# Hybrid attention block on one core: the second pass's weights in a layout of their own, and the lower right input block freed at the turn

## The chip, the cores and the metric

The kernel runs on one core of a Trainium2 chip. The metric is device time in microseconds (us) of one execution; lower is better. Engines are named as the profile names them: PE is TensorE's matmul, PEld its weight load, DVE is VectorE, ACT ScalarE, POOL GpSimd, and SP is SyncE, whose queue issues all of the DMAs that this text is about. A queue is worked off in order: an instruction that waits holds up all that stand behind it on its engine.

## What is computed

One layer of a streaming encoder, batch 1, 2048 positions, model width 1024, all in float32. Of the reference, what matters here is the first product; everything behind it uses its pieces:

```
xn = rms_norm(h, norm_gain[layer])
proj = xn @ w_in[layer]
qa, ka, va, ga, qb, kb, vb, gb, iq, ik, iw, za, zb = jnp.split(proj, offsets, axis=-1)
ya = chunked_relpos_attention(qa, ka, va, rel_bias[layer]) * jax.nn.silu(ga)
yb = dsa_sparse_attention(qb, kb, vb, iq, ik, iw) * jax.nn.silu(gb)
merged = gate_a * (ya @ w_branch_a[layer]) + gate_b * (yb @ w_branch_b[layer])
h = h + merged @ w_out[layer]
```

`x` is 2048 by 1024 and `w_in` some 5,500 columns wide. The branches a (banded attention) and b (top-256 attention) follow, and an output product.

## The kernel before

**Arithmetic.** Every float32 factor is split into a high part (rounded to the PE's fp32r) and a low part, and a product is three matmuls: high by high, high by low, low by high (`mm3`, L218 records them all). The split costs an ACT copy and a subtraction on DVE or POOL for each tile of weights.

**Stages.** Up to about 600 us the first half of the columns, the normalisation and the index branch run. From about 610 us to about 1090 us follow the *seven-product units*: 18 units (`quads`) of 256 output columns, each for the two remaining groups of 512 positions. The input is seen as a 2 by 2 matrix of blocks, A11, A12 (one group of positions, lower and upper half of the 1024 inputs), A21, A22 (the other group), and the weights of a unit as 2 by 2 blocks too. Seven block products in place of eight give the result. A block product is four slices `k` of three matmuls, 12 matmuls of 128x128 by 128x512.

- The **first pass** (`prep_one`, `first_half`) does four products of every unit, with A11, A21, A12 and A22, and keeps three sums of each unit in DRAM (`qD`).
- At the **turn** the input blocks are combined in place: A21 becomes A22 minus A21 (four slices, within the last unit of the first pass), then A22 becomes A21 plus A11 (four slices), both on PE (`combine_pe`, L1239: four matmuls by plus or minus the identity into PSUM, an ACT copy for the high part at L1241, a DVE subtraction for the low part at L1242). A12 becomes A12 minus A21 on POOL, DVE and ACT (`combine`, L1218 to L1222).
- The **second pass** (`prep_two`, `load_sums`, `part`) does three products of every unit, 36 matmuls, adds the sums from DRAM (L1367) and stores results (`evac`, L692, L698, L719).

**Weights on their way.** Per unit and slice `k` the four 128x128 blocks come by DMA to a staging tile (`wst` or `wst2`, four to five buffers), POOL combines them in place (L1260 to L1262, or L1349 and L1350), ACT writes the high part (L1248), DVE the low part (L1249). DRAM holds the weights as `wP[unit, half of the columns, 128, 8 row tiles, 128]`; a staging tile takes two DMAs, one for each half of the columns. In the second pass only three blocks are needed, one from the first half (L1347, 64 KB) and two from the second (L1348, 128 KB).

**Memory.** The second pass's pool `w2` (the sums `part`, tags p0 to p2 with two buffers each; the weights `wt2`, three buffers; staging `wst2`, four) is opened where pool `xA` and the first pass's weights lay. `xA` holds one input block, A11, so whatever lies there waits until A11 has been read for the last time, by the fourth slice of A21 plus A11. With two buffers for each sum, the sum of unit n can only be loaded when that of unit n-2 has been stored.

**Order.** The program text gives dependencies and a rough order; the order on each engine is then set by a list scheduler at build time, so an edit moves instructions that it doesn't name. After the second pass come the attention units (`a_unit`, `b_unit`), of which the first few are interleaved with the last units of the second pass, then the branch products and the output product.

## Time and profile before

| | us |
|---|---|
| median of 3 runs (2096.8 to 2107.16) | 2101.71 |
| the profiled execution | 2098.61 |
| its span, first to last instruction | 2096.8 |
| PE busy in it | 2000.5 (95%) |
| ACT, DVE, POOL busy | 1267.2, 1479.2, 804.8 |
| DMA queues' packets, share of 16 engines | 55.8% |

PE is busy 95% of the span, so what can be won is mostly the 5% in which it waits, and the stretches in which its clock was granted below full. Both are gathered in a few places, which the windows of the profile show. A busy PE in these rows also covers matmuls stretched by the low clock or by the start after an idle time, so the number of matmuls in a window, times the pitch of an undisturbed row of them, says better what was lost.

### The profile page before, as it was taken

The numbers are of one execution on the slowest core, as the hardware profiler recorded it, in microseconds if no ns is written. First come the engines' busy times: TensorE is split into PE (matmuls) and PEld (weight loads), VectorE is DVE, ScalarE is ACT, GpSimd is POOL, SyncE is SP. The second block draws the span as 40 slices with busy tenths as digits, with TensorE's granted clock in tenths as the row PEclk, the third lists the DMA queues.
The fourth block names the chain that finished last, engine by engine and source line by source line (L and its number), as shares of the span: only waits on it lengthen the run. The fifth ranks groups of instructions, "written<-read, shape, count | busy, mean of one in ns | idle before, by whom it ended". The sixth has DMA issues, their size and how long they took to land.

```text
span 2096.8 us, 34363 instructions
## 1 busy us (share of the span) xinstructions
PE 2000.5 (95%) x10674; PEld 1687.6 (80%) x10674; DVE 1479.2 (71%) x3646; ACT 1267.2 (60%) x2484; POOL 804.8 (38%) x1043
## 2 busy tenths in 40 slices
PE   8799999999999999999888999999999999999998
PEld 7588878889889877766666888888888898887886
DVE  6748887969789986565456668766885688775444
ACT  5456565565566563344567678867896698873221
POOL 2122223321142455444324455445444544443410
PEclk9899999999999999999999999999999999999999
DMA  9473345364464665478889764556346632145642
GB/s 354 150 233 130 119 133 168 115 208 152 161 209 130 221 208 187 150 245 276 253 288 252 221 212 149 182 187 216 111 133 191 212 119 68 56 138 185 215 141 91
DMA packets 310541, 375.78 MB, mean 179 GB/s; under 512 B 34384, under 2 KB 185296, under 8 KB 310224
## 3 DMA queue, kind: packets, MB, share of 16 engines
q1 hardware_dynamic: 310352, 373.54, 55.8%
q8 instruction: 85, 1.39, 0.3%
q14 instruction: 104, 0.85, 0.1%
HBM read 252.88 MB, written 120.55 MB: 178 GB/s over the span
## 4 chain that ended last, share of the span: by engine, by line
PE 43%; DMA 7%; ACT 3%; DVE 3%; issue 2%; POOL 2%; SPq 1%; DVEq 0%; POOLq 0%; ACTq 0%
PE po L1432 8%; PE d L218 7%; PE O L1015 6%; PE s L990 5%; PE pt L1007 5%; PE acc L218 4%; PE O L925 3%; PE pt L915 2%; PE s L880 2%; DMA wst<-wP 2%; DMA dst<-wB 1%; DMA dst<-wA 1%; DVE P L811 1%; DMA bias<-biasD 0%; DMA sg<-gAD 0%
## 5 line engine op out<-in xcount | busy, mean ns | idle before, releaser
L218 PE MATMUL acc<-xh,wt 128*128 128x512 f32 x2160 | 700.2, 397 | 22.9 <-ACT wt L1248 12.3
L218 PEld LDWEIGHTS acc<-xh,wt 128*128 128x128 f32 x2160 | 405.5, 189 | 126.3 <-ACT wt L1248 19.2
L218 PE MATMUL acc<-xl,wt 128*128 128x512 f32 x1080 | 425.1, 394 | 0.0
L832 POOL TENSOR_TENSOR ptl<-pf,pth 128x512 fp32r<-128x512 f32 (+1 forms) x144 | 179.7, 1248 | 207.4 <-ACT pf L828 146.8
L218 PEld LDWEIGHTS acc<-xl,wt 128*128 128x128 f32 x1080 | 204.2, 189 | 43.2
L835 DVE TENSOR_TENSOR ptl<-pt,pth 128x512 fp32r<-128x512 f32 (+1 forms) x288 | 187.5, 660 | 50.9 <-ACT pth L834 50.1
L210 POOL TENSOR_TENSOR wt<-wst,wt 128x512 fp32r<-128x512 f32 (+1 forms) x92 | 118.0, 1309 | 270.3 <-ACT wt L209 241.7
L487 DVE SCALAR_TENSOR_TENSOR sc<-lg,iw,sc 128x512 f32<-128x512 f32 (+2 forms) x266 | 178.9, 679 | 42.8 <-ACT lg L482 37.6
L990 PE MATMUL s<-kBt,qsB 128*128 128x512 f32 (+3 forms) x640 | 187.7, 383 | 1.0 <-DVE mx L811 0.7
L482 ACT ACTIVATE lg<-lg 128x512 f32<-128x512 f32 (+2 forms) x304 | 149.8, 524 | 63.7 <-PE lg L480 62.2
L834 ACT ACTIVATE pth<-pt 128x512 fp32r<-128x512 f32 (+1 forms) x288 | 160.7, 578 | 26.3 <-PE pt L1007 13.3
L1007 PE MATMUL pt<-ident,P 128*128 128x128 f32 x1088 | 165.4, 273 | 1.0 <-DVE ptl L835 0.5
L993 ACT ACTIVATE P<-P,mx 128x128 f32<-128x128 f32 (+15 forms) x128 | 154.4, 1209 | 19.5 <-DVE mx L811 19.2
L1015 PE MATMUL O<-pth,vBt 128*128 128x256 f32 x544 | 146.9, 288 | 4.0 <-ACT pth L834 1.9
L1015 PE MATMUL O<-ptl,vBt 128*128 128x256 f32 x544 | 148.0, 298 | 1.2 <-POOL ptl L832 0.8
L811 DVE CUSTOM_DVE_ANT_0 P<-s,mk,mx 128x512 f32<-128x512 f32 (+2 forms) x192 | 125.2, 652 | 32.0 <-PE s L990 25.3
L1007 PEld LDWEIGHTS pt<-ident,P 128*128 128x128 f32 x1088 | 128.3, 141 | 9.2 <-ACT pf L828 1.4
L1248 ACT ACTIVATE wt<-wst 128x512 fp32r<-128x512 f32 (+1 forms) x144 | 76.4, 571 | 94.2 <-POOL wst L1350 48.8
L1053 POOL TENSOR_TENSOR dw<-dst,dw 128x512 fp32r<-128x512 f32 x64 | 83.2, 1301 | 124.9 <-ACT dw L1052 112.8
L1249 DVE TENSOR_TENSOR wt<-wst,wt 128x512 fp32r<-128x512 f32 (+1 forms) x144 | 95.2, 684 | 48.7 <-ACT wt L1248 43.1
L880 PE MATMUL s<-kk,qs 128*128 128x320 f32 (+1 forms) x448 | 108.3, 339 | 7.5 <-DVE mx L811 4.6
L218 PE MATMUL d<-ya,dw 128*128 128x512 f32 x384 | 108.2, 407 | 6.2 <-ACT dw L1052 5.8
(274 smaller groups left out, 4453.8 us busy)
## 6 DMA issues: line engine op xcount, KB each, us to landing
wst<-wP SPq DMA_DIRECT2D x224, 128.0 KB
wst<-wP SPq DMA_DIRECT2D x84, 256.0 KB
qs<-qA SPq DMA_DIRECT2D x128, 128.0 KB
kk<-kA SPq DMA_DIRECT2D x56, 256.0 KB
vs<-vA SPq DMA_DIRECT2D x56, 256.0 KB
qD<-q SPq DMA_DIRECT2D x54, 256.0 KB
part<-qD SPq DMA_DIRECT2D x54, 256.0 KB
bias<-biasD SPq DMA_DIRECT2D x32, 320.0 KB
```

Of the source, the lines that this page charges most:

```text
L218: nc.tensor.matmul(acc, a, b, start=(first and i == 0), stop=(last and i == n - 1), **({} if first and last else {"skip_group_check": True}))
L482: nc.scalar.activation(lg, lg, AF.Relu)
L487: nc.vector.scalar_tensor_tensor(o_, lg, wv, o_, op0=OP.mult, op1=OP.add)
L832: nc.gpsimd.tensor_tensor(lo, pf, f32(hi), op=OP.subtract)
L834: nc.scalar.activation(hi, src, AF.Copy)
L835: nc.vector.tensor_tensor(lo, src, f32(hi), op=OP.subtract)
L880: nc.tensor.matmul(s_ps[:, :w], q[:, m, j * 128:(j + 1) * 128], kk[:, ko:ko + w], start=(m == 0), stop=(m == 1))
L990: nc.tensor.matmul(s_ps[:, :w], q[:, h, :], kBt[:, m, a:a + w], start=(m == 0), stop=(m == 1))
L993: nc.scalar.activation(P[:, e, :n], P[:, e, :n], AF.Exp, bias=mx[:, e:e + 1], scale=-1.0, accum_out=st["sum"][:, (u % 2) * 2 + e:(u % 2) * ...
L1007: nc.tensor.transpose(pt[:, k, e, :], P[:, e, (kt + k) * 128:(kt + k + 1) * 128], ident)
L1015: nc.tensor.matmul(o_, vBt[:, kt + k, :], src[:, k, :], start=(kt + k == 0 and n_ == 0), stop=(kt + k == b and n_ == 1), skip_group_check= ...
L1432: nc.tensor.matmul(accs[t, hf], a, b[:, n_], start=(k == 0 and i == 0), stop=(k == KT - 1 and i == 2))
```

## The change

Three things are done together.

1. A second copy of the seven-product units' weights is laid out on the host, `wS[unit, slice k, 128, 4 blocks, 128]`: what one staging tile takes is 128 rows of 2 KB, side by side, in the order block 1, 0, 2, 3 of before. One DMA fills a staging tile in the first pass, and one of 128 rows of 1.5 KB (the last three blocks) in the second.
2. The pool `xA`, whose place is given up at the turn, holds A22 in place of A11. A21 plus A11 is written over A11, and the second product of the second pass reads A11 for A22.
3. The four slices of A21 plus A11 stand behind `part(0, 0)`, the first product of the second pass, in the text, and no longer ahead of opening `w2`.

```diff
-    parts = {(s, h, z): (apool if s + h == 0 else xpool).tile([128, 4, 512], F32R, name=f"x{z}{s}{h}")
+    parts = {(s, h, z): (apool if s + h == 2 else xpool).tile([128, 4, 512], F32R, name=f"x{z}{s}{h}")
...
-            for c in range(2):
-                nc.sync.dma_start(st[:, 2 * c:2 * c + 2], io["wP"][u, c, :, k::4, :])
+            nc.sync.dma_start(st, io["wS"][u, k])
             e.tensor_tensor(st[:, 2], st[:, 3], st[:, 2], op=OP.subtract)
-            e.tensor_tensor(st[:, 3], st[:, 2], st[:, 0], op=OP.add)
-            e.tensor_tensor(st[:, 3], st[:, 1], st[:, 3], op=OP.subtract)
+            e.tensor_tensor(st[:, 3], st[:, 2], st[:, 1], op=OP.add)
+            e.tensor_tensor(st[:, 3], st[:, 0], st[:, 3], op=OP.subtract)
...
-        product(a, W, 0, A11, True, False)
+        product(a, W, 1, A11, True, False)
...
-        product(a, W, 1, A12, False, True)
+        product(a, W, 0, A12, False, True)
...
-            nc.sync.dma_start(st[:, 0:1], io["wP"][u, 0, :, k:k + 1, :])
-            nc.sync.dma_start(st[:, 1:3], io["wP"][u, 1, :, k::4, :])
+            nc.sync.dma_start(st, io["wS"][u, k, :, 1:4])
...
-        mm3(acc, [((W[z][:, 0, k], W[z][:, 1, k]), (A21, A22, A12)[z](k)) for k in range(4)], z == 0, z == 2)
+        mm3(acc, [((W[z][:, 0, k], W[z][:, 1, k]), (A21, A11, A12)[z](k)) for k in range(4)], z == 0, z == 2)
...
-    for k in range(4):
-        combine_pe(A22, A21, A11, 0, k, 2)
     a_st.close()
...
     part(0, 0)
+    for k in range(4):
+        combine_pe(A11, A21, A11, 0, k, 2)
```

**Where the order moves: ACT at the turn.** Names: `xh10` is A21's high part, `xh11` A22's, `xh00` A11's, `xh01` A12's; `wt2` are the second pass's weights, numbered by unit. ACT before:

```order
L1241 ACTIVATE xh10_146<-cm_8981 128x512
L1221 ACTIVATE xh01_144<-ct_9163 128x512
L1241 ACTIVATE xh11_148<-cm_9021 128x512
L1241 ACTIVATE xh11_148<-cm_9042 128x512
L1241 ACTIVATE xh11_148<-cm_9035 128x512
L1248 ACTIVATE wt2_9065<-wst_9066 128x3x128
L1248 ACTIVATE wt2_9065<-wst_9073 128x3x128
L1248 ACTIVATE wt2_9065<-wst_9080 128x3x128
L1248 ACTIVATE wt2_9065<-wst_9087 128x3x128
L1248 ACTIVATE wt2_9094<-wst_9095 128x3x128
```

and ACT now:

```order
L1241 ACTIVATE xh00_142<-cm_9048 128x512
L1221 ACTIVATE xh01_144<-ct_9076 128x512
L1248 ACTIVATE wt2_8965<-wst_8966 128x3x128
L1248 ACTIVATE wt2_8965<-wst_8972 128x3x128
L1248 ACTIVATE wt2_8965<-wst_8978 128x3x128
L1248 ACTIVATE wt2_8965<-wst_8984 128x3x128
L1248 ACTIVATE wt2_8990<-wst_8991 128x3x128
L1241 ACTIVATE xh10_146<-cm_8909 128x512
L1241 ACTIVATE xh00_142<-cm_9055 128x512
```

The five copies that make the first weights of the second pass stood behind all eight combined slices; now they stand ahead of the last slice of A21 (`cm_8909`) and the last two of A11.

**PE at the same place.** `cm` is a combined slice in PSUM, `acc_9123` and `acc_9015` are the first product of the second pass. PE before:

```order
L1239 MATMUL cm_9042<-xl00_143,unit_8958 128x512
L1239 MATMUL cm_9035<-xh10_146,unit_8958 128x512
L1239 MATMUL cm_9035<-xl10_147,unit_8958 128x512
L1239 MATMUL cm_9035<-xh00_142,unit_8958 128x512
L1239 MATMUL cm_9035<-xl00_143,unit_8958 128x512
L218 MATMUL acc_9123<-xh10_146,wt2_9065 128x512
L218 MATMUL acc_9123<-xl10_147,wt2_9065 128x512
```

and PE now:

```order
L1239 MATMUL cm_9055<-xl00_143,unit_8886 128x512
L1239 MATMUL cm_9062<-xh10_146,unit_8886 128x512
L218 MATMUL acc_9015<-xh10_146,wt2_8965 128x512
L218 MATMUL acc_9015<-xl10_147,wt2_8965 128x512
L218 MATMUL acc_9015<-xh10_146,wt2_8965 128x512 x2
L218 MATMUL acc_9015<-xl10_147,wt2_8965 128x512
L218 MATMUL acc_9015<-xh10_146,wt2_8965 128x512 x2
L218 MATMUL acc_9015<-xl10_147,wt2_8965 128x512
L218 MATMUL acc_9015<-xh10_146,wt2_8965 128x512 x2
L218 MATMUL acc_9015<-xl10_147,wt2_8965 128x512
L218 MATMUL acc_9015<-xh10_146,wt2_8965 128x512
L1239 MATMUL cm_9062<-xl10_147,unit_8886 128x512
```

The twelve matmuls of the first product stood behind the last combined slice; now they stand between the first and the second matmul of that slice.

**SP's queue in the second pass.** `part` are the sums, loaded from `qD` and later stored from the same tile to `sBD`, `sAD`, `kA` and others. SP before, from the stores of the sixth and seventh unit on:

```order
L698 DMA sBD2_96<-part_9541 128x512
L1357 DMA part_9704<-qD4_112 128x512
L1357 DMA part_9705<-qD4_112 128x512
L1347 DMA wst2_9729<-wP 128x128
L1348 DMA wst2_9729<-wP 128x2x128
L1357 DMA part_9706<-qD4_112 128x512
L719 DMA kA3_67<-eh_9723 128x512
L719 DMA kA3_67<-part_9621 128x512
L1347 DMA wst2_9736<-wP 128x128
L1348 DMA wst2_9736<-wP 128x2x128
L1347 DMA wst2_9743<-wP 128x128
L1348 DMA wst2_9743<-wP 128x2x128
```

and SP now, at the like place:

```order
L1355 DMA part_9598<-qD4_112 128x512
L719 DMA kA3_67<-part_9517 128x512
L698 DMA sAD3_93<-part_9597 128x512
L1355 DMA part_9680<-qD5_113 128x512
L1355 DMA part_9757<-qD6_114 128x512
L1346 DMA wst2_9701<-wS 128x384
L1346 DMA wst2_9707<-wS 128x384
L719 DMA kA2_66<-eh_9674 128x512
L1346 DMA wst2_9713<-wS 128x384
L1346 DMA wst2_9719<-wS 128x384
L719 DMA kA2_66<-part_9518 128x512
L698 DMA sAD3_93<-part_9679 128x512
```

A unit's weights take four places in place of eight, and the loads of sums have moved closer to the stores that free their tiles: before, `part_9706` takes the home of `part_9541`, five places behind that one's store; now `part_9680` and `part_9757` take the homes of `part_9517` and `part_9597`, each two places behind the store.

## Rows read from the trace of the kernel before

**Rows 1.** The page: each engine's busy time, share of the span, instructions.
```profile
PE 2000.5 (95%) x10674; PEld 1687.6 (80%) x10674; DVE 1479.2 (71%) x3646; ACT 1267.2 (60%) x2484; POOL 804.8 (38%) x1043
```

**Rows 2.** Windows: stretch, its length, busy us (and instructions) of engines.
```profile
core 0: us, PE busy (x) PEld busy (x) DVE busy (x) ACT busy (x) POOL busy (x), PEclk, DMA share, GB/s
600.00:870.00 270.00, 262.23 (x1286) 221.40 (x1285) 214.39 (x471) 137.64 (x246) 132.34 (x235) 0.99 0.59 192
870.00:910.00 40.00, 33.12 (x121) 23.62 (x120) 30.68 (x44) 14.31 (x27) 15.60 (x22) 0.91 0.44 145
910.00:1020.00 110.00, 102.26 (x425) 79.23 (x423) 56.23 (x91) 48.37 (x84) 45.94 (x92) 0.98 0.84 266
1020.00:1105.00 85.00, 71.33 (x321) 53.15 (x322) 44.31 (x107) 59.57 (x116) 27.11 (x40) 0.96 0.89 276
1105.00:1180.00 75.00, 63.82 (x368) 53.50 (x368) 46.55 (x153) 55.08 (x155) 34.30 (x41) 0.93 0.94 248
1180.00:2097.00 917.00, 893.19 (x5427) 777.93 (x5425) 624.29 (x1677) 609.66 (x1186) 399.69 (x366) 1.00 0.49 155
```

**Rows 3.** Timeline of PE at the turn: start, length, instruction, idle before it.
```profile
879.65 0.40 PE L1239 MATMUL cm<-xh,unit 128*128 128x512 f32 x1
...
894.09 0.47 PE L218 MATMUL acc<-xh,wt 128*128 128x512 f32 x1 [1.50 <-ACT wt L1248]
...
902.59 0.50 PE L218 MATMUL acc<-xh,wt 128*128 128x512 f32 x1 [1.22 <-ACT wt L1248]
```

**Rows 4.** Timelines of ACT and SP at the turn.
```profile
893.12 2.17 ACT L1248 ACTIVATE wt<-wst 128x384 fp32r<-128x384 f32 x5
892.39 2.88 SPq L1357 DMA_DIRECT2D part<-qD  x6
```

**Rows 5.** Timeline of SP in the second pass.
```profile
915.29 1.24 SPq L1357 DMA_DIRECT2D part<-qD  x2
...
945.29 0.38 SPq L1347 DMA_DIRECT2D wst<-wP  x1
945.71 0.55 SPq L1348 DMA_DIRECT2D wst<-wP  x1
947.13 0.33 SPq L1357 DMA_DIRECT2D part<-qD  x1
...
1008.90 2.10 SPq L1357 DMA_DIRECT2D part<-qD  x2
```

**Rows 6.** Waits of SP's queue from 910 to 1020 us: total, times, longest.
```profile
SPq L1357 <- DMA sBD<-part: 2.7, 4, 0.9
SPq L1357 <- DMA sAD<-part: 2.5, 3, 2.0
SPq L1357 <- DMA qB<-part: 1.9, 2, 1.1
...
SPq L1357 <- DMA kA<-part: 1.1, 1, 1.1
```

**Rows 7.** The chain that ended last, in order of time: start, us, what.
```profile
924.15 2.93 DMA sBD<-part
...
971.29 3.87 DMA kA<-part
...
999.75 4.73 DMA sAD<-part
...
1005.88 3.06 DMA wst<-wP
...
1009.10 0.47 POOL wst L1349
...
1010.13 0.53 ACT wt L1248
...
1989.29 99.17 PE po L1432 x432
```

**Rows 8.** Windows again: the first 50 us, columns as in group 2.
```profile
0.00:50.00 50.00, 42.16 (x244) 37.18 (x244) 30.16 (x70) 29.81 (x62) 10.40 (x110) 1.00 0.94 351
```

## What the change would do, predicted before it ran

> **What bounds the kernel now.** I read the page's busy line first, to see which engine could set the time at all. PE is busy 95% of the span, DVE 71%, ACT 60% [rows 1]. PE does the same matmuls after the change as before, since the seven products and the eight combined slices stay. So only time in which PE waits, or runs at a low clock, can be won. The windows say where that is [rows 2]. The last one, from 1180 us to the end, has PE busy 893.19 of 917 us at a clock of 1.00, on attention and output products, and the change does not touch them. From 600 to 870 us, the first pass, PE is busy 262.23 of 270. The three windows between are worse: 33.12 of 40 at the turn (clock 0.91), 102.26 of 110 in the second pass (clock 0.98), 71.33 of 85 in its end. That is about 7, 8 and 14 us of idle time, and none is on PE's own account.
>
> The turn, first. PE's timeline shows eight combined slices from 879.65 us on and then the first product at 894.09, which waited 1.50 us for its weights on ACT, and the second at 902.59, which waited 1.22 for the same [rows 3]. SP's timeline gives the reason: the first loads into the new pool start at 892.39 [rows 4], when A11 has been read for the last time, and every weight of the second unit is queued behind them.
>
> The second pass, next. A unit needs 36 matmuls. An undisturbed row of the same shape late in the kernel took 99.17 us for 432 [rows 7], which is 0.23 us each, so PE needs 8.3 us for a unit. SP's timeline shows pairs of loads of sums at 915.29 and at 1008.90, and ten units lie between [rows 5]: 93.61 / 10 = 9.36 us. So something holds each unit 1.1 us longer than PE needs. SP's row of issues is nearly unbroken there: two DMAs of a weight tile at 945.29 and 945.71 take 0.38 and 0.55 us, the next load of a sum 0.33 [rows 5], and SP's waits, nearly all for stores to land so that a load may take their tile, are 2.7, 2.5, 1.9 and 1.1 us in the whole window, 8.2 of 110 [rows 6]. The chain that ended last goes the same way: it runs through landings of stores (2.93, 3.87, 4.73 us), then a weight DMA of 3.06, a POOL subtraction of 0.47 and an ACT copy of 0.53 [rows 7]. I therefore read the pass as bound by SP's queue, not by the amount of data: the windows have the DMA engines at 266 GB/s and a share of 0.84 there [rows 2], and the first 50 us reached 351 GB/s at 0.94 [rows 8].
>
> **The change part by part.** *Weights in one DMA, second pass.* A unit issued four pairs, 4 x (0.38 + 0.55) = 3.7 us of SP [rows 5]. Now it issues four single DMAs of 128 rows. No row shows such a DMA for three blocks. The nearest are the two that it replaces: 0.38 for 128 rows of one block and 0.55 for 256 pieces [rows 5]. I take 0.47, the middle, so 1.9 us a unit, and keep 1.5 (4 x 0.38) and 2.2 (4 x 0.55) for the range. SP's own work falls by 1.5 to 2.2 us a unit, 1.8 by my value, so from 9.36 less its waits of 8.2/11 = 0.7 (eleven to twelve units lie in the window) = 8.6 to 6.8 us.
>
> That is not the new period, since the loads of sums now stand two to five places behind the stores that free their tiles, where they stood 5, 11 or 17 behind. Each load then waits until its store has landed. I followed the new order of SP through a unit, with 0.47 for a weight DMA, about 0.6 for a load or a store of a sum (the pair at 915.29 took 1.24 [rows 5]), and a landing time for the stores. The landing is the unknown; the chain shows 2.93, 3.87 and 4.73 [rows 7]. With 3.3 us I get 7.75 us a unit, with 3.9 I get 8.6, with 4.7 I get 9.7. The same walk through the order of before gives 9.1 at 3.3 and 9.6 at 3.9, and 9.36 was measured, so the stores of this window land in between, about 3.6. Now PE's 8.3 is the other bound, so the unit takes 8.3 to 8.6; I take 8.6 to 8.7 and a gain of 0.7 us. Twelve units run undisturbed by the turn and by the attention units: 12 x 0.7 = **8 us**, with 0 (the waits eat all) and 13 (all twelve at 8.3, 12 x 1.06) as ends. What is late next is PE itself, or the landing of a store.
>
> *The turn.* Before, the new pool opens when A11 has been read by the eighth slice, at 892.39, 12.7 us after the first slice at 879.65 [rows 3, 4]. Now it opens when A22 has been read by the fourth slice of A21, about half of that: loads, and all the weights of the second unit queued behind them, start some 6.4 us sooner. The four slices of A21 plus A11 no longer delay the weights, and the first product runs among them. On the other side PE gets a new wait: its order puts the first product between the first and second matmul of A21's last slice, and that slice's copy on ACT is behind five copies of weights, 2.17 us together [rows 4]. So PE may stand about 2.2 us, and whatever waits behind it waits too. Where PE stands, the clock can fall to its low level, 1.2 GHz, as in this window already (0.91 granted on the mean [rows 2]): 0.09 of 40 us, twice, is up to some 7 us of stretch that can appear in another place or go. I take **6 us** of gain, and 2 (6.4 less twice 2.2) to 9 (the 6.4 with the waits of 1.50 and 1.22 [rows 3] gone as well) as ends.
>
> *The end of the second pass, 1020 to 1105 us.* The same queue and stores, with the first attention units' loads mixed in; PE is idle 13.7 us, at a DMA share of 0.89 [rows 2]. Four fewer issues for each of the last units, but nearly full transfers: I take **2 us**, ends 0 and 6 (six units by 1.06).
>
> *The handover, 1105 to 1180 us.* PE is busy 63.82 of 75, at a DMA share of 0.94 [rows 2]; this is the loads of the first attention units, whose bytes are the same. If the second pass ends earlier, the same loads come due earlier, and part of the lead is lost here. I take **2 us of loss**, ends 0 and 6.
>
> *First pass.* The two DMAs of a staging tile become one here as well, but PE is busy 262.23 of 270 us [rows 2], and what is left of its waiting is not on SP. I count it at nothing, and what hides it is PE's own work; ends 1.5 us either way. *A second layout of the weights* is made on the host and read instead of the first: the same bytes. *The swap of A22 and A11* gives each product and each combined slice the same operands in size: nothing.
>
> **Sum**, against the profiled execution of 2098.61: -6 - 8 - 2 + 2 = -14 us, 2084.6. That execution is 3.1 us under the median of 2101.71, so against the median the forecast is **2088 us** (0.7% less).
>
> One rule of the Trainium skill speaks against the large term. It is worked out as the second rival below.
>
> **The rivals.** (A) *The waits take the place of the issues.* In the second pass SP's time freed by single DMAs is spent waiting for stores, as the closer order allows. This holds from a landing time of about 4.4 us on, where the walk through the new order gives 9.36 us a unit; the 4.73 of a store on the chain [rows 7] speaks for it, the 2.93 and 3.87 against. Then only the turn pays: 2101.7 - 6 = 2096.
>
> (B) *The transfers bind, and issues were hidden anyway.* A DMA share of 0.84 to 0.89 [rows 2] is not far from the 0.94 of the first 50 us [rows 8], and if the bursts around the stores fill the engines, fewer issues for the same bytes bring nothing; again the turn alone pays, 2096. Against it: SP hardly waits for anything but a store (8.2 of 110 us [rows 6]), and the 266 GB/s are well under 351. The Trainium skill ("DMA: Bandwidth & Descriptors", section "Issuing engines are not separate DMA queues") states such a rule: the time on the sequencer to initiate a DMA is usually small relative to the DMA itself. By that rule the second pass gains 0 in place of 8; the rows here have issues that fill SP's queue, and I weight it by them.
>
> (C) *Slower.* The closer order makes a store's landing part of every unit, and landings grow: loads and stores come in tighter bursts, as a share nearer to 1 makes them. By the walk a landing of 5.5 us gives 10.9 us a unit, 1.5 more than 9.36; over twelve units +18, less the turn's 6: +12, 2114. It decides from about 5.4 us for the 0.5% named below, above every landing on the chain [rows 7], which is why its chance is small.
>
> (D) *The lead is lost at the start of attention.* The second pass gains as forecast, but the window from 1105 us, with its share of 0.94 [rows 2], is bound by loads that come no sooner: -16 + 11 leaves some -5, 2097.
>
> (E) *The change does not do what it says.* One DMA of 1.5 KB rows could take SP as long as the pair that it replaces, 0.93 us. Then the second pass keeps its issues and gets the closer waits on top: about the turn's gain less 3, 2099.
>
> **How the numbers follow.** Differences within 0.5%, some 10.5 us, are about what a measurement of this kernel can tell from no change. The forecast has 0.56, with a range of its own from 2078 to 2094; A 0.20, B 0.08, C 0.07, D 0.06, E 0.03. The low end of the range, 2078, is turn 9 + second pass 13 + end 2 = 24 off; the high end, 2100, takes in A, B, D and E and leaves C out. Faster by over 0.5% (under 2091) holds nearly all of the forecast, save its upper edge, and a little of the others' lower edges: 0.54. Slower (over 2112): C and a little for a turn with the clock down: 0.08. Within: 0.38.
>
> **What would show it right or wrong.** Right: the first load into the new pool comes about 6 us after the first combined slice, not 12.7; SP's rows in the second pass have one weight DMA of about 0.47 us per tile; the distance between the loads of consecutive units falls to about 8.6 us; SP's waits on stores rise to something like 20 us over the pass while PE's idle time in it falls under 2 of 100. Rival A would show SP's waits up by as much as its issues are down, with the period still near 9.4. B would show a period near 9.4, weight DMAs landing later than 3.06 and a share above 0.9. C would show stores landing over 5 us and PE waiting more than now. D would show PE's idle time after 1105 us well above 11 of 75. The sum would be wrong altogether if the stages before 870 or after 1180 us changed by more than a microsecond or two, since I count them as untouched.

## The result

The changed kernel took 2083.33 us (median of 7 runs, 2078.6 to 2090.14) beside 2102.03 us of the kernel before: a ratio of 0.9913, 95% interval 0.9891 to 0.9936. Measured a second time it was 0.990 (0.9882 to 0.9917). That is 18.7 us less; the forecast was 14 less, 2088, in a range from 2078 to 2100.

The page's busy line of the changed kernel answers to [rows 1]: PE does the same 10674 matmuls, is 9 us shorter in them, and is busy 96% of a span of 2079.8 us.

```profile
PE 1991.3 (96%) x10674; PEld 1687.3 (81%) x10674; DVE 1474.2 (71%) x3646; ACT 1266.7 (61%) x2484; POOL 799.7 (38%) x1043
```

The windows of the changed kernel, over the same stretches as [rows 2]. Columns: stretch, length, busy us (and instructions) of PE, its weight loads, DVE, ACT, POOL, then granted clock, DMA share, GB/s.

```profile
600.00:870.00 270.00, 264.73 (x1307) 223.90 (x1306) 214.73 (x474) 139.96 (x248) 128.45 (x240) 0.99 0.60 195
870.00:910.00 40.00, 34.63 (x139) 26.40 (x137) 34.33 (x52) 19.38 (x35) 18.84 (x26) 0.96 0.49 169
910.00:1020.00 110.00, 102.23 (x430) 79.71 (x428) 54.50 (x97) 46.83 (x84) 43.15 (x88) 0.98 0.89 284
1020.00:1105.00 85.00, 71.35 (x369) 58.05 (x368) 50.19 (x133) 70.18 (x155) 34.02 (x43) 0.96 0.99 299
1105.00:1180.00 75.00, 70.55 (x406) 60.11 (x406) 48.15 (x146) 54.51 (x140) 37.27 (x45) 0.95 0.82 238
1180.00:2097.00 917.00, 873.51 (x5299) 760.84 (x5297) 609.55 (x1641) 593.69 (x1149) 387.84 (x355) 0.99 0.48 149
```

Read the counts in brackets, not the busy times. From 1020 to 1105 us PE is busy for the same 71.3 us as before, but gets 369 matmuls done where it did 321, and the DMA engines carry 299 GB/s at a share of 0.99 where they carried 276 at 0.89.

Because the work moves under fixed windows, a second reading is needed: the time at which the same instruction starts in both traces. ACT does nearly the same 2480 instructions in every kernel here, so the n-th copy of each kind was paired with the n-th of the kernel before; the table gives the median difference over 20 us (minus: earlier than before), at places named by the time in the kernel before. Each row is one execution, so a row can differ from its kernel's median: that of e4 is the slowest of six, that of e6 the fastest of twelve.

| kernel | 600 | 860 | 900 | 1000 | 1120 | 1280 | 2000 |
|---|---|---|---|---|---|---|---|
| changed | +0.5 | -4.0 | -10.0 | -14.1 | -23.1 | -20.0 | -17.0 |
| changed, second time (e9) | +1.2 | -4.5 | -10.3 | -13.0 | -24.4 | -26.1 | -24.5 |
| layout alone (e1) | +0.8 | -5.7 | -4.8 | -11.2 | -19.6 | -20.5 | -20.1 |
| turn alone (e2) | +0.5 | -1.2 | -6.2 | -1.0 | +0.6 | -1.9 | -2.9 |
| first pass alone (e3) | +0.8 | -2.9 | -2.9 | -3.2 | -1.1 | -1.9 | -2.4 |
| second pass alone (e4) | +1.9 | +1.0 | +1.7 | -3.8 | -10.6 | -10.2 | -9.3 |
| small pieces (e5) | -0.6 | -9.3 | -15.0 | -15.0 | -21.9 | -24.3 | -24.7 |
| two halves (e6) | +0.5 | -4.5 | -9.0 | -6.3 | -6.0 | -8.8 | -10.5 |
| sums from ACT (e7) | +0.1 | -6.4 | -11.0 | -16.6 | -26.7 | -30.0 | -28.2 |
| layout, sums from ACT (e10) | +0.7 | -3.9 | -3.2 | -3.2 | -7.3 | -13.1 | -13.7 |
| before, sums from ACT (e11) | +0.2 | -1.0 | -0.9 | -2.9 | -2.6 | -5.2 | -5.5 |
| layout alone, small pieces (e12) | +0.2 | -6.2 | -6.5 | -10.2 | -19.5 | -21.6 | -20.1 |

Three things gain time in the changed kernel: the first pass (4.5 us by 860), the turn (6 us by 900) and the second pass with its end (13 us by 1120). Some of it goes again behind 1120 us, and more in one execution than in the other. At 900 the table flatters the turn, because the copies of weights that the new order moves ahead on ACT are among the instructions paired. PE's matmuls, paired in the same way, start 8.1 us earlier at 900, 13.6 at 1000 and 22.5 at 1120 (the second time 8.5, 13.0 and 24.2); at 860 and from 1280 on they agree with the table.

**The turn in the trace of the changed kernel.** PE's timeline, first combined slice, then the two waits that the new order brings:

```profile
875.67 0.40 PE L1239 MATMUL cm<-xh,unit 128*128 128x512 f32 x1
...
884.64 0.50 PE L1239 MATMUL cm<-xh,unit 128*128 128x512 f32 x1 [1.58 <-ACT xh L1241]
887.88 0.79 PE L218 MATMUL acc<-xh,wt 128*128 128x512 f32 x1 [2.74 <-DVE xl L1242]
```

and SP's timeline at the same place:

```profile
881.70 2.69 SPq L1355 DMA_DIRECT2D part<-qD  x6
884.50 16.32 SPq L1346 DMA_DIRECT2D wst<-wS  x11
```

The first load into the new pool starts 6.0 us after the first combined slice, where it took 12.7 [rows 3, 4]. But the eleven weight DMAs behind it, which need about 5 us of issuing, take 16.32: SP now waits there for staging tiles to come free.

**SP's waits in the second pass**, 910 to 1020 us (total, times, longest), beside [rows 6]:

```profile
SPq L1355 <- DMA sAD<-part: 12.7, 8, 3.0
SPq L1355 <- DMA sBD<-part: 8.7, 7, 2.1
SPq L1346 <- DVE wt L1249: 6.9, 10, 1.3
SPq L1355 <- DMA kA<-part: 6.1, 4, 2.8
SPq L1355 <- DMA qB<-part: 3.6, 3, 1.9
```

The four rows that name a store make 31.1 us, where they made 8.2. The other side is SP's time for a weight DMA: shortest, median and longest in ns, from 910 to 1020 us, first the two DMAs of a tile in the kernel before, then the single one of the changed kernel.

```profile
L1347 SPq DMA_DIRECT2D wst<-wP x46: 337/543/610, 911.2 to 1016.6; - x46
L1348 SPq DMA_DIRECT2D wst<-wP x47: 550/551/1525, 909.7 to 1017.2; - x47
```

```profile
L1346 SPq DMA_DIRECT2D wst<-wS x42: 327/382/502, 910.1 to 1019.9; - x42
```

By the medians a tile took SP 1.09 us and takes 0.38 now: four tiles a unit, 4.4 us and 1.5.

**How long a unit takes.** Since the work moves, the ten units are set beside each other from the start of the second pass's 73rd matmul to that of its 433rd, ten times 36 matmuls: the kernel before, then the changed kernel.

```profile
915.40:1009.10 93.70, 87.08 (x361) 67.69 (x360) 48.94 (x78) 39.59 (x70) 39.61 (x80) 0.98 0.85 270
```

```profile
907.30:995.50 88.20, 84.88 (x362) 66.84 (x361) 45.24 (x77) 36.80 (x66) 37.04 (x77) 1.00 0.90 294
```

A unit on PE takes 8.82 us in place of 9.37 (8.92 the second time), and PE's idle time over the ten falls from 6.6 to 3.3 us. By the loads of sums on SP, of which thirty lie between these two, it is (990.78 - 906.81) / 10 = 8.40 beside the 9.36 of before:

```profile
906.81 0.32 SPq L1355 DMA_DIRECT2D part<-qD  x1
...
990.78 0.44 SPq L1355 DMA_DIRECT2D part<-qD  x1
```

The window from 910 to 1020 us hides this (430 matmuls beside 425, the same idle time), since in the changed kernel two waits of PE of 3.7 us in all, behind the ten units, fall into it.

### The profile page after: what moved, and what is told of

It is laid out like the page before. It is cut to its first block, busy times and chain, and to the rows that moved or that the text cites. A ratio compares the mean times of both kernels' runs of the same rounds, so it can differ in the third digit from the quotient of the medians.

```text
span 2079.8 us, 34128 instructions
## 1 busy us (share of the span) xinstructions
PE 1991.3 (96%) x10674; PEld 1687.3 (81%) x10674; DVE 1474.2 (71%) x3646; ACT 1266.7 (61%) x2484; POOL 799.7 (38%) x1043
## 4 chain that ended last, share of the span: by engine, by line
PE 40%; DMA 9%; DVE 3%; issue 2%; ACT 2%; POOL 2%; SPq 1%; DVEq 0%; POOLq 0%; ACTq 0%
PE po L1430 6%; PE d L218 6%; PE O L1015 6%; PE acc L218 5%; PE s L990 5%; PE pt L1007 5%; PE O L925 3%; PE s L880 2%; PE pt L915 2%; DMA dst<-wB 2%; DMA dst<-wA 1%; DMA mf<-mD 1%; DMA wst<-wS 1%; DVE P L811 1%; POOL dw L1053 1%
## 5 line engine op out<-in xcount | busy, mean ns | idle before, releaser
L218 PE MATMUL acc<-xh,wt 128*128 128x512 f32 x2160 | 697.0, 395 | 17.5 <-ACT wt L1248 7.5
L834 ACT ACTIVATE pth<-pt 128x512 fp32r<-128x512 f32 (+1 forms) x288 | 160.3, 577 | 25.4 <-PE pt L1007 13.1
L811 DVE CUSTOM_DVE_ANT_0 P<-s,mk,mx 128x512 f32<-128x512 f32 (+2 forms) x192 | 125.3, 652 | 32.1 <-PE s L990 25.7
L990 PEld LDWEIGHTS s<-kBt,qsB 128*128 128x128 f32 x640 | 102.5, 189 | 14.5 <-DVE mx L811 6.5
```

Source lines behind the costliest of these rows:

```text
L218: nc.tensor.matmul(acc, a, b, start=(first and i == 0), stop=(last and i == n - 1), **({} if first and last else {"skip_group_check": True}))
L811: nc.vector.tensor_tensor_reduce(dst, ps_, add, 1.0, FMAX if first else mx, OP.add, OP.min, accum_out=mx)
L834: nc.scalar.activation(hi, src, AF.Copy)
L990: nc.tensor.matmul(s_ps[:, :w], q[:, h, :], kBt[:, m, a:a + w], start=(m == 0), stop=(m == 1))
```

## The experiments

My theory was S: the number of DMAs that SP must issue holds the second pass, and its end, and single DMAs free it. The rivals: the waits take the place of the issues (A), the transfers bind (B), and, once the result was there, P: the size of the pieces (512 B before, 1.5 KB after) is what unloads the DMA engines.

**The change taken apart.** The layout in both passes with the turn of before, as a diff against the changed kernel:

```diff
-    parts = {(s, h, z): (apool if s + h == 2 else xpool).tile([128, 4, 512], F32R, name=f"x{z}{s}{h}")
+    parts = {(s, h, z): (apool if s + h == 0 else xpool).tile([128, 4, 512], F32R, name=f"x{z}{s}{h}")
...
+    for k in range(4):
+        combine_pe(A22, A21, A11, 0, k, 2)
     a_st.close()
...
     part(0, 0)
-    for k in range(4):
-        combine_pe(A11, A21, A11, 0, k, 2)
```

> The new layout with one DMA per staging tile in both passes; the turn as before (A11 gives up its place, the four slices of A21 plus A11 stand ahead of the second pass). My theory (SP's issues hold the second pass): the stretch from 905 to 1000 us gains about 4 us, its end some 4 more, the first pass the 4 us seen in the changed kernel: about 2102 - 10 = 2092 (2088 to 2096). Rival B (transfers bind, issues were hidden): only what the first pass gives, 2097 or more, and a distance of about 9.4 us between the units' loads of sums. SP's waits for stores to land rise from 8 us to about 30 in 910 to 1020 us by my theory.

Measured: 2079.92 us beside 2099.25, a ratio of 0.9912 (0.9896 to 0.9928). This one part gives as much as the whole change, and more than I expected of it (2088 to 2096). SP's waits on stores came to 37.1 us, as expected.

The turn alone, weights by two DMAs as before (against the kernel before; A22's place and the operand of part z=1 go with it):

```diff
-    for k in range(4):
-        combine_pe(A22, A21, A11, 0, k, 2)
     a_st.close()
...
     part(0, 0)
+    for k in range(4):
+        combine_pe(A11, A21, A11, 0, k, 2)
```

> The turn alone: A22 gives up its place, the four slices of A21 plus A11 stand behind the first product of the second pass; weights by two DMAs a tile as before. My theory: the first load of a sum comes some 6 us sooner after the first combined slice, and the total is about 2102 - 6 = 2096 (2093 to 2100), with no lead gained before 860 us. Rival: the parts only work together (the lead is lost again in a second pass bound by SP's queue): 2100 to 2102. A second rival: the turn alone carries most of the gain, 2088 or less.

Measured: 0.9990 (0.9979 to 1.0002), about 2 us less and not told from nothing. The lead is there at 900 us, -6.2, and gone by 1000. Its SP timeline shows where most of it stops being of use:

```profile
895.53 0.55 SPq L1348 DMA_DIRECT2D wst<-wP  x1
901.70 0.33 SPq L1347 DMA_DIRECT2D wst<-wP  x1
```

Between these two, SP issues nothing for 5.6 us. The row of its waits from 891 to 972 us names what for: the low parts on DVE, which free the staging tiles.

```profile
SPq L1347 <- DVE wt L1249: 7.3, 6, 5.5
```

So the pool opens sooner, SP runs ahead until its staging tiles are full, and stands. The total fits the first rival, that the lead is lost again in a second pass bound by SP's queue, and lies at the near edge of my own range too; the table decides for the rival. Why the units after that take longer here than before (9.72 us on PE in place of 9.37; the lead shrinks from 6 us at 900 to 1 at 1000) is not settled: the build-time scheduler also set another order.

The first pass alone, with the turn of before (the two blocks that swap places go with it):

```diff
-            for c in range(2):
-                nc.sync.dma_start(st[:, 2 * c:2 * c + 2], io["wP"][u, c, :, k::4, :])
+            nc.sync.dma_start(st, io["wS"][u, k])
```

> The new layout and one DMA per tile in the first pass alone (A11's and A12's blocks swap places there); second pass and turn as before. If the 4 us that the changed kernel gains before 860 us come from weights that arrive sooner at the switch near 823 us, this kernel has them too: PE's wait of 2.66 us on the weights' low part gone, no low clock behind it, total about 2098 (2096 to 2100). Rival: they come from another order that only the whole change brings (an accident of the order): the wait stays and the total is 2101 to 2103.

and the second pass alone:

```diff
-            nc.sync.dma_start(st[:, 0:1], io["wP"][u, 0, :, k:k + 1, :])
-            nc.sync.dma_start(st[:, 1:3], io["wP"][u, 1, :, k::4, :])
+            nc.sync.dma_start(st, io["wS"][u, k, :, 1:4])
```

> The new layout and one DMA per tile in the second pass alone; first pass and turn as before. My theory: distance between the units' loads of sums down from 9.4 to about 8.8 us, SP's waits for stores up to some 30 us between 910 and 1020 us, total about 2102 - 7 = 2095 (2091 to 2099). Rival A (waits take the place of the issues): distance 9.4, total 2101 to 2103. Rival B (transfers bind): the same distance and total, but SP's waits unchanged near 8 us and weight DMAs that land later. Rival C (stores land later than 5 us): distance over 10, total over 2106.

Measured: 0.9971 (0.9957 to 0.9984), some 6 us, for the first pass, and 0.9933 (0.9917 to 0.9949), some 14 us, for the second. Their product, 0.9904, is the layout's 0.9912 within the intervals: they add up. The second pass alone gave twice the 7 us that I expected, with 8.87 us from load to load (expected 8.8) and 38.2 us of waits on stores (30); the first pass alone lies at the upper edge of the 2 to 6 us that I had.

The first pass has one place. PE's timeline of the kernel before, which I had read and, rightly, not thought to be SP's:

```profile
828.32 0.74 PE L218 MATMUL acc<-xh,wt 128*128 128x512 f32 x2 [2.66 <-DVE wt L1249]
```

PE waited 2.66 us for the low part of a weight, which DVE writes. DVE at this place in the kernel before, and ACT, which writes the high parts of the same weights:

```profile
819.56 0.15 DVE L584 TENSOR_SCALAR flag<-lg 1x1 int32<-1x1 f32 x1 [2.02 <-PE lg L582]
822.53 0.69 DVE L1285 TENSOR_TENSOR q<-acc,q 128x512 f32<-128x512 f32 x1 [2.82 <-PE acc L218]
827.58 2.16 DVE L1249 TENSOR_TENSOR wt<-wst,wt 128x512 fp32r<-128x512 f32 x3 [4.35 <-issue]
```

```profile
822.58 2.20 ACT L1248 ACTIVATE wt<-wst 128x512 fp32r<-128x512 f32 x4 [4.12 <-PE acc L218]
```

and DVE with the layout in the first pass alone:

```profile
820.07 0.14 DVE L584 TENSOR_SCALAR flag<-lg 1x1 int32<-1x1 f32 x1 [3.96 <-PE lg L582]
825.81 0.69 DVE L1284 TENSOR_TENSOR q<-acc,q 128x512 f32<-128x512 f32 x1 [5.59 <-PE acc L218]
826.42 1.89 DVE L1249 TENSOR_TENSOR wt<-wst,wt 128x512 fp32r<-128x512 f32 x3
```

ACT had the weights by 822.58 us in the kernel before, so their DMAs were not late. DVE was. `flag` decides a branch of the program (`tc.Switch`, from L585 on, in the index search), and from the branch's last instruction, which ends at 823.67, DVE runs nothing until 827.58. In the kernel before its order has `q`, a sum that waits for a product of PE, ahead of that branch and the low parts of the weights behind it. With one DMA a tile the scheduler has put `q` behind the branch: DVE passes the branch while it would have to wait for PE anyway, and the low parts follow `q` at once. All four kernels with two DMAs a tile in the first pass (before, e2, e4, e11) have the first order and the wait, 2.5 to 2.66 us; all with one DMA have the second order, and the wait is gone. From 600 to 860 us the table has 0.9 to 1.7 us gained in e2, e4 and e11 and 3.7 to 8.7 in the nine rows with one DMA. So most of the first pass's gain comes from one place in DVE's order, and not from weights that arrive sooner. What I expected of e3 came (the wait is gone), but not for the reason that I gave.

Behind the wait PE went on at the low level, 1.2 GHz, for part of the stretch. The windows from 800 to 820 and from 820 to 840 us, in the kernel before:

```profile
800.00:820.00 20.00, 18.34 (x80) 14.25 (x79) 17.42 (x30) 6.39 (x10) 12.82 (x22) 1.00 0.63 211
820.00:840.00 20.00, 17.34 (x69) 13.69 (x68) 6.21 (x9) 5.14 (x10) 9.71 (x20) 0.91 0.47 154
```

and with the layout in the first pass alone:

```profile
800.00:820.00 20.00, 17.84 (x74) 13.99 (x72) 14.91 (x28) 5.38 (x8) 12.42 (x22) 0.91 0.65 228
820.00:840.00 20.00, 19.07 (x85) 15.33 (x84) 7.63 (x13) 6.07 (x11) 6.16 (x15) 1.00 0.50 166
```

In e3 the low clock, which I expected to go, has moved: a wait of 2.16 us for ACT at 813.80 has it behind itself. The same holds in e6 (2.06 us at 812.26, a clock of 0.91 from 800 to 820). In the changed kernel, e1 and e12 the wait at that place is 1.75, 1.18 and 1.88 us and the clock stays at 1.00.

**Issues or pieces.** The changed kernel with one DMA a tile, as many issues in the same order, but the second pass's weights laid out by blocks, so that a DMA has 384 pieces of 512 B:

```diff
-            nc.sync.dma_start(st, io["wS"][u, k, :, 1:4])
+            nc.sync.dma_start(st, io["wQ"][u, k, 1:4].rearrange("b p n -> p b n"))
```

> The changed kernel with the second pass's weights laid out so that one DMA still fills a staging tile, but of 384 pieces of 512 B (the size of before) in place of 128 of 1.5 KB; the order of all engines stays that of the changed kernel. Theory S (the number of issues on SP made the gain): 2080 to 2087 beside 2102 of before, as the changed kernel, unless the issue itself takes much longer than 0.38 us. Theory P (the size of the pieces made it, because the DMA engines are full from 1000 us on): most of the second pass's 13 us is gone, 2090 to 2097, weight DMAs land later and the stretch from 1020 to 1105 us falls back by 5 us or more.

Measured: 0.9899 (0.9883 to 0.9915). Theory P falls by the total, and all engines kept the order of the changed kernel. But the table shows the first pass of this kernel, which is the changed kernel's to the instruction, 5 us ahead at 860, and from 900 to 1120 a gain of only 7 us in place of 13. So the same was done to the kernel of the layout alone:

> The kernel of the new layout alone (turn as before, ratio 0.9912) with the second pass's weights in 384 pieces of 512 B for each DMA in place of 128 of 1.5 KB, and the order of all engines as in that kernel. In the first trial of small pieces the first pass happened to end 5 us sooner than in its pair, so the second pass's own share stayed open. If the number of issues alone counts: ratio 0.990 to 0.9925, and from 900 to 1120 us some 13 to 15 us of lead are gained against the kernel before, as with large pieces. If the size of the pieces counts too, since the DMA engines' share is 0.98 and more behind 1020 us: 0.9935 to 0.997, and only 6 to 9 us are gained there.

Measured: 0.9908 (0.9885 to 0.9930) beside 0.9912 with large pieces, and from 900 to 1120 us 13.0 us of lead gained beside 14.8. The pages show that the pieces are small again: packets of this kernel, then of the changed one.

```profile
DMA packets 280586, 375.75 MB, mean 181 GB/s; under 512 B 32080, under 2 KB 146128, under 8 KB 280272
```

```profile
DMA packets 262154, 375.75 MB, mean 181 GB/s; under 512 B 32080, under 2 KB 127696, under 8 KB 261840
```

18432 more packets, and no difference in the total. SP's time for a weight DMA in this kernel:

```profile
L1346 SPq DMA_DIRECT2D wst<-wQ x43: 383/411/590, 909.7 to 1007.7; - x43
```

A median of 0.41 us beside 0.38: 384 small pieces issue nearly as fast as 128 large ones. The stage itself does show the pieces. Counted as above, a unit on PE takes 9.18 us in e5 and 9.13 in e12, where it takes 8.82 to 8.92 in the four executions with one DMA of large pieces (changed, e9, e1, e4). From the third unit to the last, PE gains 9.8 us in e5 and 10.0 in e12, and 12.0 to 14.7 in those four. So small pieces cost some 2 to 5 us of the second pass in both pairs; the totals, with intervals of 4 us either way, neither show nor exclude that.

The other way round, the large pieces, but two issues a tile:

```diff
-            nc.sync.dma_start(st, io["wS"][u, k, :, 1:4])
+            for c in (0, 64):
+                nc.sync.dma_start(st[c:c + 64], io["wS"][u, k, c:c + 64, 1:4])
```

> The changed kernel with each staging tile of the second pass filled by two DMAs of 64 rows of 1.5 KB: eight issues a unit, as before, but large pieces. Theory S: the gain of the second pass is lost, 2093 to 2098, and the distance between the units' weights is 9.2 us or more. Theory P: the gain stays, 2080 to 2088. If both count, 2088 to 2093.

Measured: 2092.71 beside 2096.89, 0.9974 (0.9963 to 0.9985). All but 5 us are gone, which is about what the first pass gives. A unit on PE takes 9.43 us, and 9.45 from load to load, as Theory S expected (9.2 or more). SP's time for a weight DMA:

```profile
L1347 SPq DMA_DIRECT2D wst<-wS x87: 471/582/1399, 909.4 to 1010.3; - x87
```

0.58 us for a DMA of half the bytes, eight a unit, so 4.7 us of SP where the kernel before had 4.4 and the changed kernel has 1.5. SP's waits on stores are small again (910 to 1020 us), 1.8 us in all beside 8.2 in the kernel before:

```profile
SPq L1356 <- DMA qB<-part: 0.9, 2, 0.8
SPq L1356 <- DMA sAD<-part: 0.5, 2, 0.4
SPq L1356 <- DMA sBD<-part: 0.4, 1, 0.4
```

Together these three runs show theory S for the larger part of the second pass: with bytes and layout equal, going back to two issues takes some 13 to 15 us away; with issues and order equal, small pieces change the total by nothing that can be told and the stage by 2 to 5 us. One thing is not separated: the scheduler sets SP's order by the number of DMAs, so e6 has both more issues and another order, with the loads further from their stores. That the closer order alone could bring the gain is not shown, and its waits on stores (31 to 38 us in place of 8) speak against it.

**What the waits on stores still cost.** The loads of the sums taken off SP's queue, to ACT's (shown) and to POOL's (`nc.gpsimd`):

```diff
-            nc.sync.dma_start(f32(second[q][1][z]), qD[quads[q]][(2, 1, 0)[z]])
+            nc.scalar.dma_start(f32(second[q][1][z]), qD[quads[q]][(2, 1, 0)[z]])
```

> The changed kernel with the loads of the second pass's sums issued from ACT in place of SP, so that a load that waits for its store to land no longer holds up the weights on SP (it may hold up ACT's copies instead). If the remaining 31 us of SP's waits on stores (910 to 1020 us) still cost time: faster than the changed kernel by 2 to 6 us, about 2079. If PE or the DMA engines bind by now: 2083 within 2 us. If the waits only move to ACT, which makes the weights: slower, 2088 or more, with ACT waiting for stores.

> The same with the loads of the sums issued from POOL, which combines the weights' blocks. If SP's waits on stores still cost time: about 2079. If PE or the DMA engines bind: 2083 within 2 us. If the waits move to POOL's queue, ahead of the subtractions that every weight needs, or the issue takes POOL over 1 us: 2088 or more.

Measured: from ACT 0.9875 (0.9858 to 0.9892), from POOL 0.9907 (0.9891 to 0.9922). The first is the fastest kernel of the study, 2070.62 beside 2096.89, though its interval touches those of the changed kernel (0.9913 and 0.990), and they did not run side by side. Its window and the largest wait of SP's queue in the same stretch:

```profile
910.00:1020.00 110.00, 106.00 (x454) 83.63 (x452) 56.00 (x97) 52.08 (x92) 48.51 (x94) 0.98 0.92 308
```

```profile
SPq L1346 <- DVE wt L1249: 26.1, 19, 3.0
```

SP now waits for free staging tiles, so it has become early, and PE gets 454 matmuls done in place of 430, at 308 GB/s. That speaks against a limit of the DMA engines at the 284 GB/s of the changed kernel.

The changed kernel was run again beside two more kernels that load the sums from ACT by the same edit, one on the kernel of the layout alone and one on the kernel before:

> The changed kernel once more, unaltered, beside the next two on one chip, so that they can be set against it. Every theory expects the ratio of the first comparison, 0.991 (0.989 to 0.994).

> The new layout with one DMA per tile in both passes and the sums of the second pass loaded from ACT, with the turn of the kernel before. It differs from the changed kernel with sums from ACT (ratio 0.9875) by the turn alone. If the turn's 5 us are lost in the changed kernel only because SP's queue waits for stores anyway, they show here: this kernel is 3 to 6 us slower than that one, a ratio of 0.989 to 0.9905. If the turn is worth nothing where loads do not hold up weights either: 0.9865 to 0.9885.

> The kernel before with nothing changed but the queue of the sums' loads: ACT issues them. SP loses three issues a unit (about 1.3 us) and its 0.7 us of waits on stores, as many us as the single weight DMAs take from it. Theory S (SP's queue bounds the second pass of the kernel before): faster by 8 to 14 us, a ratio of 0.993 to 0.996, without any new layout. If the layout itself made the gain: 1.000 within 0.002. If ACT's queue is held up by the stores: over 1.002.

Measured: for the changed kernel 0.990, as told above; for the other two 0.9952 (0.9937 to 0.9968) and 0.9985 (0.9967 to 1.0002). Both of these miss what I expected. With the old turn, loads from ACT cost 8 us against the layout alone, and in the kernel before they bring at most 7 in place of 8 to 14. ACT's waits in e10, 860 to 1020 us, show why such a load is not free:

```profile
ACT wt L1248 <- DMA part<-qD: 7.8, 2, 5.3
ACT wt L1248 <- DMA sAD<-part: 6.1, 2, 3.1
```

Copies of weights stood behind loads that waited for stores; 13.9 us in 160. That it pays in e7 and not in e10 lies in where the two orders put the loads on ACT's queue, or so I argue (in e7 the same two kinds of wait make 5.1 us); no run here separates it, since each edit brings its own order. e11 came out where I had put the rival that the layout itself makes the gain (1.000 within 0.002). In it ACT's copies of weights wait 6.0 us for a load and a store to land, and PE waits 10.6 us for those copies from 860 to 1020 us, as long as in the kernel before: some of what came off SP's queue went onto the engine that makes the weights. So e11 lends S no support, and S rests on e6 and on the pairs of e5 and e12. And e7 beside e10 differ by the turn alone and by 16 us, far more than the 3 to 6 I had set: with the loads on ACT the turn, or the order that it brings, does matter.

## Why the prediction was right, point by point

**The bound.** That the second pass hung on SP's queue more than on the bytes was right, by e6 and by the totals of e5 and e12. My reading of SP's waits was not: I called them nearly all waits for stores, 8.2 us, but left out the two largest rows, and together the rows that wait for an engine make 12.6 us more of the 110.

```profile
SPq L1347 <- DVE part L1367: 3.1, 8, 0.6
SPq L698 <- ACT wt L1248: 3.1, 9, 0.6
```

So SP was held by staging tiles and copies too, and not only by its issues and the stores. The rule of the Trainium skill that I weighed as rival B ("DMA: Bandwidth & Descriptors", section "Issuing engines are not separate DMA queues": the time to initiate a DMA is usually small relative to the DMA) agrees with each single DMA here, 0.55 us of issue beside 3.06 us for the weight DMA on the chain [rows 7]. What I drew from it, a gain of nothing, did not come: the issues stand one behind the other on one queue, and four more a unit cost some 14 us in all.

| stage | forecast | by ACT's starts (two executions) | by PE's |
|---|---|---|---|
| first pass | 0 | -4.5, -5.7 | -4.5, -5.7 |
| turn, 860 to 900 | -6 | -6.0, -5.8 | -4.1, -4.0 |
| second pass, 900 to 1000 | -8 | -4.1, -2.7 | -5.5, -4.5 |
| its end, 1000 to 1120 | -2 | -9.0, -11.4 | -8.9, -11.2 |
| behind 1120 | +2 | +6.1, -0.1 | +5.5, -0.3 |
| sum | -14 | -17.5, -25.7 | -17.5, -25.7 |

**Weights in one DMA.** I took 0.47 us an issue and 0.93 for the pair that it replaces, each from one row; the medians are 0.38 and 1.09. So SP got back 2.8 us a unit where I had 1.8. Rival E, that a single DMA issues as slowly as the pair, is out.

**The loads' waits.** I expected SP's waits on stores to rise to some 20 us; they rose to 31, about 1.7 us a unit. So rival A did take place in part, and it is luck that it and the cheaper issue nearly cancel: 2.8 - 1.7 leaves 1.1 us a unit, and 8.40 us from load to load was measured where I had 8.6. PE got less of it, 0.55 us a unit in place of 0.7, or 5.5 us over the ten units. Its idle time did not fall under 2 of 100 us, as I had named for a sign, but to 3.3 of 88. Rival C did not come; the units did not get longer than before.

**The end of the second pass.** This is the term that I mis-sized: 2 forecast with an end at 6, 9 to 11 measured. I argued that nearly full transfers (a share of 0.89) would not let more through. The window shows 299 GB/s at 0.99 where it had 276 at 0.89. With two halves (e6) this gain is absent (-6.3 at 1000, -6.0 at 1120; 270 GB/s at 0.88 in the window), so it goes with the issues and the order that they bring: SP's queue held the transfers back there as well, in the mix with the first attention units.

**The turn.** Its size at 900 us was right by ACT's starts, -6, but PE had only 4 us of it; the window from 870 to 910 us agrees, 18 more matmuls of 0.23 us. Of the two new waits of PE that I had at about 2.2 us each at most, one was shorter and one longer, 1.58 and 2.74. What was wrong is that I counted the turn to the end. I had named what comes next for the second pass but not for the turn: SP, released 6 us sooner, fills the staging tiles and waits for them (16.32 us for eleven DMAs). With the loads of the sums on SP the totals leave the turn 0 to 3 us: e2 beside the kernel before has 2, and the changed kernel beside e1 0 and, the second time, 2 to 3, each with an interval of some us. Where the lead goes is settled only for e2, by 1000 us. From 860 to 1120 us the changed kernel's two executions gain 19.1 and 19.9 us where e1 gains 13.9, so there the turn still shows at 1120; but e5 and e12, which differ by the turn alone too, gain 12.6 and 13.3. With the loads on ACT (e7 beside e10) the turn, or the order that comes with it, is worth 16 us.

**The first pass.** I counted it at nothing because "what is left of its waiting is not on SP". That reason was right, and the number was wrong all the same: the wait of 2.66 us lay on DVE, behind a branch, and it went because the scheduler moved one sum of DVE from ahead of the branch to behind it. I had no term for what another order brings in a stage whose own bound the change does not touch.

**Behind 1120.** By the sign that I had named, PE idle well above 11 of 75 us from 1105 us on, rival D did not come: it is 4.5 us idle in one execution and 3.0 in the other. The first lost some of its lead all the same, and the other did not. The window from 1105 to 1180 us of the second one, beside 70.55 and a clock of 0.95 above:

```profile
1105.00:1180.00 75.00, 71.98 (x435) 60.73 (x433) 52.96 (x161) 59.13 (x150) 38.71 (x46) 1.00 0.81 236
```

The first had waits of PE of 2.9 and 1.59 us in this window and the low level of the clock for a while; half of its 6 us went behind 1280 us, and what took those is not settled. Since the same kernel kept its lead the second time, the 6 us are no property of the change.

In sum: that the total came out near the forecast is in part luck, because the terms missed in both directions. I had written that the sum would be wrong if the stages before 870 us changed by more than a microsecond or two, and they changed by 4.5 to 5.7. The second pass was somewhat too large, and the turn counted for 6 us of which the totals show 0 to 3; the end of the second pass and the first pass were too small. The end of the pass comes from the mechanism that I had right but did not follow far enough: SP's queue held back that stretch as well. The first pass comes from DVE's order and not from SP.

## What to carry to other kernels

When one queue issues all DMAs, add up its issues per round before its bytes: here four issues and some 2.8 us of SP's time saved in each round of 9 us were worth some 14 us, where a start moved forward by 6 us brought 0 to 3. Where a profile books a wait to an engine (here DVE), follow it back until you know what held that engine, a DMA, a branch or its order, before you put it down to the change: the first pass gained in every kernel with the new layout there, and yet not by the layout's DMAs. Before you count on a start that is moved forward, look whether the queue behind it has free buffers to run into; in e2 it had none, and the lead was gone 100 us later.

## What was not expected of the hardware

- SP took a median of 0.41 us to issue a DMA of 384 pieces of 512 B (e12), 0.38 for 128 pieces of 1.5 KB (changed kernel), but 0.58 for half of that (e6), and 0.54 and 0.55 for 128 and 256 pieces of 512 B (before). The price follows neither the pieces nor the bytes; it is lower in the kernels that issue one DMA a tile, and why is not shown.
- 18432 more packets of 512 B at a DMA share of 0.97 (1020 to 1105 us of e12, 299 GB/s) changed the total by nothing that the comparison could tell, though the units of the second pass took 0.3 us longer.
- A wait of PE does not settle the clock behind it. In the first pass waits of 2.5 to 2.66 us (before, e2, e4, e11), of 2.16 (e3) and of 2.06 (e6) have a mean clock of 0.97 over 800 to 860 us; with waits of 1.75 (changed), 1.88 (e12) and even 2.16 us (e8) it is 1.00.
